# First feed-forward products of groups 1 to 3 as seven block products per pair of jobs instead of eight

## The chip, the cores and the metric

The kernel runs on one core of one Trainium2 chip. The time is that of the device in microseconds; the kernel before took 1534.74 us in the median of 3 runs (1532.2 to 1538.27). In the profile the engines are PE (TensorE, matmuls), PEld (TensorE's loads of the stationary operand), DVE (VectorE), ACT (ScalarE), POOL (GpSimdE) and SP (SyncE, which issues the DMAs).

## The reference

The program is a two-layer trunk over 512 frames with 16 meta tokens set in front of them, so 528 tokens of width 1024. Each layer is a mixer (attention in layer 0, retention in layer 1), and then a feed-forward block with a squared ReLU between two products, each with a scaled residual and a layer norm:

```python
def _sq_relu_mlp(h, w1, w2):
    return jnp.square(jax.nn.relu(h @ w1)) @ w2

for layer in range(DEPTH):
    ...
    h = _layer_norm(DEEPNORM_ALPHA * h + mix, ln_g[layer, 0], ln_b[layer, 0])
    h = _layer_norm(DEEPNORM_ALPHA * h + _sq_relu_mlp(h, ffn_w1[layer], ffn_w2[layer]),
                    ln_g[layer, 1], ln_b[layer, 1])
return h[:, N_META:, :]
```

`w1` is 1024 x 4096 and `w2` 4096 x 1024, everything in float32. The change is in the product `h @ w1`.

## The kernel before

**Layout and precision.** Activations lie transposed: features on the 128 partitions, tokens along the columns. `hs[k]` is feature tile k of 8, as a pair of a high part `hh` and a low part `hl` whose sum is the value. Weights are split the same way, into `wh` and `wl`. Every product takes three passes (PASSES): high by high, high by low, low by high. Layer 0 works on all 528 tokens (FULL) in two halves of 264 columns, layer 1's block on 512 (S_FULL); the meta tokens are not needed after it.

**Weights.** `weight_plan` lists all 224 weight tiles of 128 x 1024 in the order of use. `prepare` (L197 to L207) takes the next one: SP loads `raw` (L203), ScalarE casts it to `wh` (L205), VectorE subtracts to get `wl` (L206). `weights` (L209) keeps this two tiles ahead of the products. The raw tiles have a pool of 3, everything else of this size shares `upool` with 44 buffers.

**The feed-forward block.** `mlp` (L1059) goes through 4 groups of 1024 hidden features. An up job takes one weight tile and yields 128 hidden features. In layer 0 it is 48 matmuls of 264 columns (8 feature tiles, 3 passes, 2 halves) into a two-bank PSUM tile `mm`, in layer 1 it is 24 matmuls of 512 columns into a `bank`. Then `squared` (L1047) applies the ReLU on ScalarE (L1052), the square to the high part `gh` on ScalarE (L1054), and on VectorE the square in full (L1055) and the low part `gl` (L1056). A down job adds one tile of the second product to `y` (L1034, L1036 for the first group). Two up jobs of the next group stand ahead of the eight down jobs of a group, so that TensorE has work while the last squares are made; six follow behind. The last group's down jobs are given to `tail`, which makes the layer norm beside them. PSUM has 2 tiles of two banks (`mm`) and 4 single banks.

**What sets the order.** A scheduler orders the instructions of each engine by the program's order and their operands; each engine then works through its own queue in that order and waits on semaphores of the others. `Ordered` (`pe`) fixes TensorE's order to that of the program where `pe.on` is set.

Of the kernel before, what the change touches and what calls it, by code (L numbers as in the profile page):

```python
# [8 lines left out]
F32 = mybir.dt.float32  # L9
# [39 lines left out]
def weight_plan():  # L49
    plan = []  # L50
    qa, ka, va, qb, kb, vb = (512 * i for i in range(6))

    def wide(name, c0):
        for kk in range(4):
            plan.append(("B", name, 0, 256 * kk, c0))

    def tall(name, c0, r0=0):
        plan.append(("A", name, 0, r0, c0))

    wide("even_w_in", va)  # L60
# [47 lines left out]
    return plan  # L108


@with_exitstack
def kernel(
# [36 lines left out]
            return self.put(nc.tensor.transpose(*a, **k))  # L149
    pe = Ordered()  # L150
    plan = weight_plan()

    cpool = ctx.enter_context(tc.tile_pool(name="cpool", bufs=1))
# [43 lines left out]
    def prepare(load=nc.sync.dma_start):  # L197
        i = queue["next"]
        if i == len(plan):
            return  # L200
        queue["next"] += 1
        raw = rpool.tile([P, 1024], F32, tag="raw", name="raw")
        load(out=raw, in_=w[i])  # L203
        wh, wl = flat(F32R, "wh"), flat(F32R, "wl")
        act.copy(out=wh, in_=raw)  # L205
        dve.tensor_tensor(out=wl, in0=raw, in1=f(wh), op=ALU.subtract)  # L206
        queue["ready"].append((wh, wl))  # L207

    def weights(kind, ahead=2):  # L209
        while queue["next"] < min(len(plan), queue["used"] + 1 + ahead):  # L210
            prepare()
        assert plan[queue["used"]][0] == kind
        queue["used"] += 1
        wh, wl = queue["ready"].pop(0)
        k, n = {"A": (8, P), "B": (2, 512), "C": (4, 256)}[kind]
        return tuple(t.rearrange("p (k n) -> p k n", k=k, n=n) for t in (wh, wl))
# [830 lines left out]
    def squared(dst):  # L1047
# [8 lines left out]
            dve.tensor_tensor(out=gl, in0=s[:, :n], in1=f(gh), op=ALU.subtract)  # L1056
        return put

    def mlp(hs, full, a, b, norm, gs, steps=LN_STEPS):  # L1059
        for g in range(NG):  # L1060
            nxt = []

            def up(into, upto):
                while len(into) < upto:
                    dst = two(F32R, "g")
                    get, run = job(hs, squared(dst))
                    run(get(), full)
                    into.append(dst)
# [4 lines left out]
            if g + 1 < NG:  # L1073
                for get, run in jobs:
                    run(get(), full)
                up(nxt, 8)
            else:
# [247 lines left out]
```

## Time and profile before

| what | number |
|---|---|
| median of 3 runs | 1534.74 us (1532.2 to 1538.27) |
| span of the profiled execution | 1538.6 us |
| stretch of layer 0's feed-forward block that the windows take | 390 to 690 us of the span |
| stretch of layer 1's feed-forward block that the windows take | 1200 to 1480 us of the span |
| weight tiles | 224, of which 64 for `ffn_w1` |

Of the profiled execution only the span is given, no time of its own beside it. The page has the busy time of each engine, the chain of work that ended last, groups of instructions and DMA issues. Rows of the timeline read: start and duration in us, engine, line, operation, result and operands, shape, and in brackets the idle time of the engine before it with what ended that. Rows that group instructions read: how many, busy us and mean ns of one, then the idle time before them with what ended most of it. Windows give the busy time of each engine in a stretch, with the number of instructions in brackets, and the granted clock of TensorE (1.00 is full).

### The profile page before, as it was taken

How to read it: one execution, taken by the hardware profiler on the slowest of the kernel's cores; microseconds unless marked ns; L12 is line 12 of the kernel's file. 1: busy time of each engine (PE TensorE's matmuls, PEld its weight loads, DVE VectorE, ACT ScalarE, POOL GpSimd, SP SyncE). 2: the span in 40 equal slices, each digit the busy share in tenths (PEclk: the TensorE clock that was granted, in tenths of full speed). 3: DMA queues.
4: the chain of work that ended last, by engine and by line, in shares of the span. 5: the costliest groups of instructions: out<-in, count | busy, mean ns of one | idle time of the engine just before them, and what ended most of it. 6: DMA issues, size and time to landing. Idle time of an engine off the chain costs nothing.

```text
span 1538.6 us, 22350 instructions
## 1 busy us (share of the span) xinstructions
PE 1514.1 (98%) x9464; PEld 1343.7 (87%) x9464; DVE 774.2 (50%) x1306; ACT 581.5 (38%) x940; POOL 0.2 (0%) x4
## 2 busy tenths in 40 slices
PE   8999999999999999999999999999999999999997
PEld 6887878799999999999988888888899888888886
DVE  4565466577514435157544354254477524435257
ACT  4474344436403224044444343153455403223133
POOL 0000000000000000000000000000000000000000
PEclk9999999899999999999999999999999999999998
DMA  6111102140302414034013135022150312414021
GB/s 241 56 52 45 56 28 85 44 149 19 129 32 83 137 44 154 31 131 135 28 35 119 36 107 168 0 77 101 46 174 28 122 57 83 137 55 165 28 83 55
DMA packets 39588, 128.97 MB, mean 84 GB/s; under 512 B 4724, under 2 KB 7172, under 8 KB 39488
## 3 DMA queue, kind: packets, MB, share of 16 engines
q1 hardware_dynamic: 39488, 127.54, 25.2%
q8 instruction: 74, 1.21, 0.3%
q14 instruction: 26, 0.21, 0.0%
HBM read 125.43 MB, written 2.10 MB: 83 GB/s over the span
## 4 chain that ended last, share of the span: by engine, by line
PE 97%; DVE 2%; ACT 0%; DMA 0%; issue 0%; ACTq 0%
PE bank L146 45%; PE mm L146 30%; PE v_ps L146 10%; PE s_ps L146 5%; PE o_ps L146 4%; PE t_ps L149 1%; PE sum_ps L146 1%; DVE y L896 0%; PE fb_ps L146 0%; PE mo_ps L146 0%; PE vm_ps L146 0%; PE ms_ps L146 0%; DMA raw<-in_w 0%; PE rows_ps L146 0%; PE sm_ps L146 0%; DVE s L293 0%
## 5 line engine op out<-in xcount | busy, mean ns | idle before, releaser
L206 DVE TENSOR_TENSOR wl<-raw,wh 128x1024 fp32r<-128x1024 f32 x224 | 271.6, 1222 | 92.4 <-ACT wh L205 84.4
L205 ACT CAST wh<-raw 128x1024 fp32r<-128x1024 f32 x224 | 230.5, 1043 | 104.3 <-DMA raw<-in_w 101.9
L146 PE MATMUL bank<-hh,wh 128*128 128x512 f32 (+3 forms) x640 | 220.9, 356 | 0.0
L146 PE MATMUL bank<-hh,wl 128*128 128x512 f32 (+3 forms) x640 | 216.5, 350 | 0.0
L146 PE MATMUL bank<-g,wh 128*128 128x512 f32 (+2 forms) x800 | 200.7, 342 | 0.0
L146 PE MATMUL bank<-hl,wh 128*128 128x512 f32 (+3 forms) x640 | 196.1, 350 | 4.1 <-DVE hl L888 4.1
L146 PEld LDWEIGHTS bank<-g,wh 128*128 128x128 f32 x800 | 137.9, 188 | 18.2
L146 PEld LDWEIGHTS bank<-hh,wh 128*128 128x128 f32 x640 | 120.9, 189 | 18.9 <-ACT hh L900 1.2
L146 PE MATMUL bank<-g,wl 128*128 128x512 f32 (+2 forms) x400 | 136.3, 341 | 0.0
L1055 DVE TENSOR_TENSOR relu<-relu 128x528 f32<-128x528 f32 (+3 forms) x76 | 46.6, 613 | 178.0 <-ACT relu L1052 178.0
L146 PEld LDWEIGHTS bank<-hh,wl 128*128 128x128 f32 x640 | 120.8, 189 | 16.8
L146 PE MATMUL mm<-g,wh 128*128 128x264 f32 x832 | 134.9, 284 | 0.0
L146 PEld LDWEIGHTS bank<-hl,wh 128*128 128x128 f32 x640 | 108.8, 188 | 22.1 <-DVE hl L888 4.7
L146 PEld LDWEIGHTS mm<-g,wh 128*128 128x128 f32 x832 | 115.0, 188 | 0.0
L146 PE MATMUL mm<-hh,wh 128*128 128x264 f32 x512 | 104.1, 285 | 0.0
L146 PE MATMUL mm<-hl,wh 128*128 128x264 f32 x512 | 104.1, 284 | 0.0
L146 PE MATMUL mm<-hh,wl 128*128 128x264 f32 x512 | 103.9, 284 | 0.0
L1052 ACT ACTIVATE relu<-bank 128x512 f32<-128x512 f32 (+2 forms) x50 | 24.7, 493 | 194.4 <-PE bank L146 194.4
L146 PE MATMUL mm<-s,wh 128*128 128x264 f32 x544 | 95.4, 298 | 0.5 <-DVE s L302 0.5
L1052 ACT ACTIVATE relu<-mm 128x528 f32<-128x528 f32 x26 | 15.9, 612 | 189.5 <-PE mm L146 189.5
L146 PE MATMUL mm<-g,wl 128*128 128x264 f32 x416 | 84.3, 284 | 0.0
L146 PEld LDWEIGHTS mm<-s,wh 128*128 128x128 f32 x544 | 77.3, 194 | 6.9 <-issue 2.3
(267 smaller groups left out, 2494.9 us busy)
## 6 DMA issues: line engine op xcount, KB each, us to landing
raw<-in_w SPq DMA_DIRECT2D x224, 512.0 KB, 3.8
xf<-in_x SPq DMA_DIRECT2D x8, 264.0 KB, 5.6
y<-in_x SPq DMA_DIRECT2D x8, 264.0 KB, 4.4
out<-y SPq DMA_DIRECT2D x8, 256.0 KB, 2.2
nb<-in_c_nb SPq DMA_DIRECT2D x4, 264.0 KB
rd<-in_c_rd SPq DMA_DIRECT2D x4, 256.0 KB
rd<-in_c_rm SPq DMA_DIRECT2D x4, 192.0 KB, 3.7
fm<-in_c_fm SPq DMA_DIRECT2D x1, 264.0 KB, 2.7
```

The lines of the kernel that those rows point to most:

```text
L146: return self.put(nc.tensor.matmul(*a, **k))
L149: return self.put(nc.tensor.transpose(*a, **k))
L205: act.copy(out=wh, in_=raw)
L206: dve.tensor_tensor(out=wl, in0=raw, in1=f(wh), op=ALU.subtract)
L1052: act.activation(out=a, in_=ps, func=AF.Relu)
L1055: dve.tensor_tensor(out=s[:, :n], in0=r[:, :n], in1=r[:, :n], op=ALU.mult)
```

## The change

Groups 1 to 3 of the up products, 12 pairs of jobs in each layer, become 12 quads in each layer. A quad takes the two weight tiles of 256 hidden features, cuts the contraction into two halves of 512, the features into two blocks of 128 and the tokens into two halves, which is a 2 x 2 by 2 x 2 block product. In place of the eight block products it makes seven by Strassen's scheme: "11", "a", "b", "12", "d", "c" and "22", each 4 feature tiles in 3 passes, 12 matmuls of 264 (layer 0) or 256 columns (layer 1). The operands "a", "b", "c" and "d" of the weights are sums made in `quad_steps` (below L225 is the subtraction for `wl`, L238 the sum s0, L244 and L246 the sum s1, L249 the low part of the block "12"); those of the tokens are differences made by `combined` once per layer, while group 0's products and down jobs run. The casts to high parts are ScalarE's. The results are put together on VectorE in v (L1163), m (L1165), L1170, L1172 and L1176, with two copies on ScalarE (L1161, L1168); then come ReLU and square in one operation (L1178, 128 x 1056 in layer 0), the cast on ScalarE (L1179) and the low part (L1180). These line numbers are of the changed kernel.

Two accumulators, of "b", "c" and "22" in bank 0 and of "d" in bank 1, share the two-bank PSUM tile `qc`. "22" and what follows it is done inside the next quad (`between`), between its "b" and its "12". One quad of the next group stands ahead of the down jobs of groups 1 and 2, so the quads of a layer run in sequences of 5, 4 and 3. The two weight tiles of a quad are loaded one quad ahead; their preparation goes on by a step after each block product. The raw tiles move to `upool`, which has 46 buffers, and their own pool goes. `pe.on` is set from the first quad to the last but the tail. Host-side packing puts the four blocks of a quad into two tiles, so that as many bytes are loaded as before.

```diff
@@ weight_plan, mlp
+        def quad(g, q):
+            plan.append(("Q", "ffn_w1", layer, 0, D * g + 2 * P * q))
         for g in range(NG):
-            if g + 1 < NG:
-                up(g + 1, 0)
-                up(g + 1, 1)
+            if g and g + 1 < NG:
+                quad(g + 1, 0)
             for f in range(KT):
                 down(g, f)
             if g + 1 < NG:
-                for f in range(2, 8):
-                    up(g + 1, f)
+                for q in range(min(g, 1), 4):
+                    quad(g + 1, q)
...
-    upool = ctx.enter_context(tc.tile_pool(name="upool", bufs=44))
-    rpool = ctx.enter_context(tc.tile_pool(name="rpool", bufs=3))
+    upool = ctx.enter_context(tc.tile_pool(name="upool", bufs=46))
...
+    def halves(raw):
         wh, wl = flat(F32R, "wh"), flat(F32R, "wl")
         act.copy(out=wh, in_=raw)
         dve.tensor_tensor(out=wl, in0=raw, in1=f(wh), op=ALU.subtract)
+        return wh, wl
+
+    def quad_steps(quad, at):
+        lo, hi = slice(0, 512), slice(512, 1024)
+        r0, r1 = flat(F32, "raw"), flat(F32, "raw")
+        nc.sync.dma_start(out=r0, in_=w[at])
+        nc.sync.dma_start(out=r1, in_=w[at + 1])
+        yield
+        h, l = halves(r0)
+        quad["11"], quad["22"] = (h[:, lo], l[:, lo]), (h[:, hi], l[:, hi])
+        yield
+        s0 = flat(F32, "sums")
+        dve.tensor_tensor(out=s0.rearrange("p (a b) -> p a b", a=2), in0=r0.rearrange("p (a b) -> p a b", a=2),
+                          in1=dup(r1[:, hi], 512), op=ALU.add)
+        yield
+        h, l = halves(s0)
+        quad["c"], quad["a"] = (h[:, lo], l[:, lo]), (h[:, hi], l[:, hi])
+        s1 = flat(F32, "sums")
+        dve.tensor_tensor(out=s1[:, lo], in0=s0[:, hi], in1=r0[:, lo], op=ALU.add)
+        yield
+        dve.tensor_tensor(out=s1[:, hi], in0=s1[:, lo], in1=r1[:, lo], op=ALU.add)
+        t = flat(F32R, "w12")
+        act.copy(out=t[:, lo], in_=r1[:, lo])
+        dve.tensor_tensor(out=t[:, hi], in0=r1[:, lo], in1=f(t)[:, lo], op=ALU.subtract)
+        quad["12"] = t[:, lo], t[:, hi]
+        yield
+        h, l = halves(s1)
+        quad["b"], quad["d"] = (h[:, lo], l[:, lo]), (h[:, hi], l[:, hi])
+
+    def advance():
+        for item in queue["ready"]:
+            if isinstance(item, dict) and next(item["steps"], item) is not item:
+                return
...
+    def combined(a, b, into):
+        (c1, n), (c2, _) = a, b
+        for j in range(2):
+            p, q = (y_t[2 * i + j] for i in range(2))
+            p1, p2, q1, q2 = (t[:, :, c:c + n] for t in (p, q) for c in (c1, c2))
+            u, v = (both(F32, "ts")[:, :, :2 * n] for _ in range(2))
+            dve.tensor_tensor(out=u[:, :, :n], in0=p2, in1=p1, op=ALU.subtract)
+            dve.tensor_tensor(out=u[:, :, n:], in0=q2, in1=u[:, :, :n], op=ALU.subtract)
+            yield
+            dve.tensor_tensor(out=v[:, :, :n], in0=p2, in1=q2, op=ALU.subtract)
+            dve.tensor_tensor(out=v[:, :, n:], in0=q1, in1=u[:, :, n:], op=ALU.subtract)
+            yield
+            for t in (u, v):
+                h, l = (both(F32R, "tc")[:, :, :2 * n] for _ in range(2))
+                act.copy(out=h, in_=t)
+                dve.tensor_tensor(out=l, in0=t, in1=f(h), op=ALU.subtract)
+                into.append((h, l))
+                yield
+
+    def quad_up(hs, ts, a, b, dst, between):
+        (c1, n), (c2, _) = a, b
+        quad = weights("Q")
...
+        def multiply(ps, name, xs, first):
+            wt = quad[name]
+            for k in range(4):
+                for i, (p, q) in enumerate(PASSES):
+                    pe.matmul(ps, lhsT=wt[p][:, P * k:P * k + P], rhs=xs[k][q], start=first and k == 0 and i == 0, skip_group_check=not first,
+                              stop=k == 3 and i == 2)
+            advance()
+
+        pa, pb, pcd = bank("qa")[:, :n], bank("qb")[:, :n], two_banks("qc")
+        pc, pd = pcd[:, 0, :n], pcd[:, 1, :n]
+        gh, gl = dst
+        tv = both(F32, "tv").rearrange("p a b -> p (a b)")
+        t, v, m = (tv[:, n * i:n * i + n] for i in range(3))
+        r = both(F32, "up")
+        one, two_ = slice(c1, c1 + n), slice(c2, c2 + n)
+        multiply(pa, "11", plain(0, c1), True)
+        act.copy(out=t, in_=pa)
+        multiply(pb, "a", mixed(0), True)
+        dve.tensor_tensor(out=v, in0=pb, in1=t, op=ALU.subtract)
+        multiply(pc, "b", mixed(1), True)
+        dve.tensor_tensor(out=m, in0=pc, in1=v, op=ALU.add)
+        between()
+        multiply(pa, "12", plain(4, c1), False)
+        act.copy(out=r[:, 0, one], in_=pa)
+        multiply(pd, "d", plain(4, c2), True)
+        dve.tensor_tensor(out=r[:, 0, two_], in0=pd, in1=m, op=ALU.subtract)
+        multiply(pc, "c", mixed(2), False)
+        dve.tensor_tensor(out=r[:, 1, two_], in0=pc, in1=v, op=ALU.add)
+
+        def finish():
+            multiply(pc, "22", mixed(3), False)
+            dve.tensor_tensor(out=r[:, 1, one], in0=pc, in1=t, op=ALU.subtract)
+            rs, hs_, ls = (x[:, :, c1:c1 + 2 * n] for x in (r, gh, gl))
+            dve.scalar_tensor_tensor(out=rs, in0=rs, scalar=0.0, in1=rs, op0=ALU.max, op1=ALU.mult)
+            act.copy(out=hs_, in_=rs)
+            dve.tensor_tensor(out=ls, in0=rs, in1=f(hs_), op=ALU.subtract)
+        return finish
...
         for g in range(NG):
             nxt = []
...
-            up(gs, 8)
-            if g + 1 < NG:
-                up(nxt, 2)
+            if g and g + 1 < NG:
+                quads(nxt, 1)
             jobs = [job(gs, add_into(y[k], ALPHA if g == 0 else None)) for k in range(KT)]
...
+            for k, (get, run) in enumerate(jobs):
+                run(get(), full)
+                if k == 0:
+                    between()
+                advance()
+                advance()
+            pe.on = True
             gs = nxt
+            quads(gs, 4 - len(gs) // 2)
```

**VectorE where layer 0's first down jobs end and the next up jobs begin, before** (`y` is the residual, `relu` is the ReLU's result, `g` a hidden tile, `raw`, `wh` and `wl` the weight tile and its parts; the waits are on semaphores of the named engine or DMA queue):

```order
L206 TENSOR_TENSOR wl<-raw,wh 128x1024 [waits DMAHW3_49,Activation_49]
L206 TENSOR_TENSOR wl<-raw,wh 128x1024 [waits DMAHW4_49,Activation_49]
L1036 SCALAR_TENSOR_TENSOR y<-y,mm 128x528 [waits PE_49]
L206 TENSOR_TENSOR wl<-raw,wh 128x1024 [waits DMAHW5_49,DVE_49,Activation_49]
L1036 SCALAR_TENSOR_TENSOR y<-y,mm 128x528 [waits PE_49] x6
L1055 TENSOR_TENSOR relu<-relu 128x528 [waits Activation_49]
L1056 TENSOR_TENSOR g<-relu,g 128x528 [waits DVE_49,Activation_49]
L206 TENSOR_TENSOR wl<-raw,wh 128x1024 [waits DMAHW6_49,Activation_49]
```

Each up job brings two operations of 528 columns (L1055, L1056), each weight tile one of 1024 (L206), and each down job one of 528 (L1036).

**VectorE in the second quad of the first sequence, after** (numbers tell the tiles apart: `qc_4852`, `tv_4853`, `up_4854`, `g_4845` belong to the first quad, `qb_4960`, `qc_4961`, `tv_4962`, `up_4963` to the second, `wl_5009`, `sums_5012`, `w12_5028`, `wl_5048` and `raw_4955`, `raw_4956` are weights of the third):

```order
L1163 TENSOR_TENSOR tv_4962<-qb_4960,tv_4962 128x264 [waits PE_49,Activation_49]
L1165 TENSOR_TENSOR tv_4962<-qc_4961,tv_4962 128x264 [waits DVE_49,PE_49]
L1176 TENSOR_TENSOR up_4854<-qc_4852,tv_4853 128x264 [waits PE_49]
L225 TENSOR_TENSOR wl_5009<-sums_4993,wh_5008 128x1024 [waits Activation_49]
L244 TENSOR_TENSOR sums_5012<-sums_4993,raw_4955 128x512
L1178 SCALAR_TENSOR_TENSOR up_4854<-up_4854 128x1056 [waits DVE_49]
L249 TENSOR_TENSOR w12_5028<-raw_4956,w12_5028 128x512 [waits Activation_49]
L246 TENSOR_TENSOR sums_5012<-sums_5012,raw_4956 128x512 [waits DVE_49]
L1180 TENSOR_TENSOR g_4845<-up_4854,g_4844 128x1056 [waits Activation_49]
L225 TENSOR_TENSOR wl_5048<-sums_5012,wh_5047 128x1024 [waits Activation_49]
L1170 TENSOR_TENSOR up_4963<-qc_4961,tv_4962 128x264 [waits PE_49]
L225 TENSOR_TENSOR wl_5102<-raw_5080,wh_5101 128x1024 [waits DMAHW7_49,Activation_49]
```

L1170, which reads the second quad's "d", stands behind the first quad's L1176, L1178 and L1180 and behind five operations on the third quad's weights; L1172, which reads "c", follows two further on.

**TensorE at the end of an up job, before** (`mm` is the accumulator; the waits are for the parts of the weight):

```order
L146 MATMUL mm<-hh,wh 128x264 x2
L146 MATMUL mm<-hl,wh 128x264 x2
L146 MATMUL mm<-hh,wl 128x264 x2
L146 MATMUL mm<-hh,wh 128x264 [waits Activation_49]
L146 MATMUL mm<-hh,wh 128x264
L146 MATMUL mm<-hl,wh 128x264 x2
L146 MATMUL mm<-hh,wl 128x264 [waits DVE_49]
L146 MATMUL mm<-hh,wl 128x264
```

Matmuls of consecutive jobs go to different accumulators and wait only for weights.

**TensorE in the second quad of the first sequence, after** (`hh`, `hl` are the tokens' parts, `tc` the tokens' differences; the rows are the last of "d" and the first of "c"):

```order
L156 MATMUL qc_4961<-hh_3332,wh_4935 128x264
L156 MATMUL qc_4961<-hl_3333,wh_4935 128x264
L156 MATMUL qc_4961<-hh_3332,wl_4936 128x264
L156 MATMUL qc_4961<-hh_3332,wh_4935 128x264
L156 MATMUL qc_4961<-hl_3333,wh_4935 128x264
L156 MATMUL qc_4961<-hh_3332,wl_4936 128x264
L156 MATMUL qc_4961<-tc_4335,wh_4899 128x264 [waits DVE_49]
L156 MATMUL qc_4961<-tc_4336,wh_4899 128x264
L156 MATMUL qc_4961<-tc_4335,wl_4900 128x264
L156 MATMUL qc_4961<-tc_4335,wh_4899 128x264
```

The first matmul of "c" waits for a VectorE count that only L1170 of this quad reaches (L1170 reads bank 1 of `qc_4961`, "c" writes bank 0), and no matmul of other work stands between "d" and "c". The first matmul of "d" waits in the same way for L1165, which reads bank 0.

More of the change, by code (lines that the diff above doesn't have):

```diff
@@ L108, in weight_plan, with plan_tiles @@
     return plan
+def plan_tiles(plan):
+    first, n = [], 0
+    for item in plan:
+        first.append(n)
+        n += 2 if item[0] == "Q" else 1
+    return first
 @with_exitstack
@@ L201, in prepare @@
         queue["next"] += 1
-        raw = rpool.tile([P, 1024], F32, tag="raw", name="raw")
-        load(out=raw, in_=w[i])
+        if plan[i][0] == "Q":
+            quad = {}
+            quad["steps"] = quad_steps(quad, first_tile[i])
+            next(quad["steps"])
+            queue["ready"].append(quad)
+            return
+        raw = flat(F32, "raw")
+        load(out=raw, in_=w[first_tile[i]])
+        queue["ready"].append(halves(raw))
+    def halves(raw):
         wh, wl = flat(F32R, "wh"), flat(F32R, "wl")
@@ L213, in weights @@
         queue["used"] += 1
+        if kind == "Q":
+            quad = queue["ready"].pop(0)
+            for _ in quad["steps"]:
+                pass
+            return quad
         wh, wl = queue["ready"].pop(0)
@@ new lines, in mlp, with between, quads @@
+    def mlp(hs, full, a, b, norm, gs, steps=LN_STEPS):
+        ts = []
+        mix = combined(a, b, ts)
+        while len(gs) < 8:
+            dst = two(F32R, "g")
+            get, run = job(hs, squared(dst))
+            run(get(), full)
+            gs.append(dst)
+            for _ in range(4):
+                next(mix, None)
+        run_all(mix)
+        left = {"finish": lambda: None}
+        def between():
+            left["finish"]()
+            left["finish"] = lambda: None
+        def quads(into, n):
+            for _ in range(n):
+                gh, gl = both(F32R, "g"), both(F32R, "g")
+                left["finish"] = quad_up(hs, ts, a, b, (gh, gl), between)
+                into += [(gh[:, i, :], gl[:, i, :]) for i in range(2)]
@@ L1258 @@
     for kind, name, layer, r0, c0 in weight_plan():
+        if kind == "Q":
+            for blocks in (((0, 0), (1, 1)), ((1, 0), (0, 1))):
+                tiles.append(np.concatenate([
+                    given[name][layer][r0 + 512 * k:r0 + 512 * k + 512, c0 + 128 * o:c0 + 128 * o + 128]
+                    .reshape(4, 128, 128).transpose(1, 0, 2).reshape(128, 512) for k, o in blocks], axis=1))
+            continue
         kt, n = {"A": (8, 128), "B": (2, 512), "C": (4, 256)}[kind]
```

25 lines of the change are left out of this document (12 added, 13 removed).

## The prediction

> **What bounds the kernel now.** I read the page first, for its span, its busy times and its chain of work that ended last.
>
> ```profile
> span 1538.6 us, 22350 instructions
> PE 1514.1 (98%) x9464; PEld 1343.7 (87%) x9464; DVE 774.2 (50%) x1306; ACT 581.5 (38%) x940; POOL 0.2 (0%) x4
> PE 97%; DVE 2%; ACT 0%; DMA 0%; issue 0%; ACTq 0%
> raw<-in_w SPq DMA_DIRECT2D x224, 512.0 KB, 3.8
> ```
>
> TensorE is busy for 98% of the span and makes up 97% of the chain. The span is the only time there is for the profiled execution, and it lies 3.9 us above the median of the runs (1534.7), about the distance of the slowest run. I therefore work out a difference against this trace and add it to the median. About 0.5%, 7.7 us, is what a measurement of this kernel can tell from no change.
>
> Then the stretches that the change touches, by the windows (the columns after the length are PE, PEld, DVE, ACT and POOL busy, then the granted clock, the DMA share and GB/s): the feed-forward part of layer 0 and that of layer 1.
>
> ```profile
> 390.00:690.00 300.00, 300.00 (x2469) 300.00 (x2468) 115.70 (x129) 82.09 (x103) 0.00 (x0) 1.00 0.27 89
> 1200.00:1480.00 280.00, 280.00 (x1212) 227.52 (x1211) 110.72 (x129) 80.14 (x105) 0.00 (x0) 1.00 0.28 91
> ```
>
> TensorE has no idle time there at all, and it has the full clock. VectorE works 39% of the time, ScalarE 27 to 29%. So a matmul removed there is worth its whole spacing, and nothing else in these stretches is late today. There is also no wait there that the change could take away: whatever waits it brings are new.
>
> **What is removed.** A pair of up jobs has 2 x 48 = 96 matmuls of 264 columns in layer 0; a quad has 7 x 12 = 84. The spacing comes from the ends of up jobs, as ScalarE's timeline shows them (start, duration, then the idle time before):
>
> ```profile
> 461.15 0.61 ACT L1052 ACTIVATE relu<-mm 128x528 f32<-128x528 f32 x1 [38.54 <-PE mm L146]
> ...
> 502.05 0.61 ACT L1052 ACTIVATE relu<-mm 128x528 f32<-128x528 f32 x1 [3.62 <-PE mm L146]
> 1271.81 0.60 ACT L1052 ACTIVATE relu<-bank 128x512 f32<-128x512 f32 x1 [36.10 <-PE bank L146]
> ...
> 1294.01 0.60 ACT L1052 ACTIVATE relu<-bank 128x512 f32<-128x512 f32 x1 [3.36 <-PE bank L146]
> ```
>
> In layer 0 these are 7 intervals in 40.90 us, 5.843 us a job, 121.7 ns a matmul. A quad then takes 84 x 0.1217 = 10.23 us for 11.69: 1.46 us less, 17.5 us for 12 quads. In layer 1, 4 intervals in 22.20 us give 5.55 us a job (24 matmuls of 512), 11.10 a pair. The 256-column matmuls that replace them appear in the tail's down jobs of 24 matmuls each:
>
> ```profile
> 1491.21 0.42 DVE L1034 TENSOR_TENSOR y<-y,bank 128x256 f32<-128x256 f32 x1 [0.57 <-PE bank L146]
> 1494.03 0.42 DVE L1034 TENSOR_TENSOR y<-y,bank 128x256 f32<-128x256 f32 x1 [2.40 <-PE bank L146]
> 1496.87 0.42 DVE L1034 TENSOR_TENSOR y<-y,bank 128x256 f32<-128x256 f32 x1 [1.23 <-PE bank L146]
> ```
>
> 2.82 and 2.84 us for 24 are 118 ns each, so 84 take 9.91 us: 1.19 less, 14.3 for 12. **Removed: 31.8 us**, 1.32 us a quad. That is the gain if TensorE never waits.
>
> **What is added, and on which engine.** The durations:
>
> ```profile
> L206 DVE TENSOR_TENSOR wl<-raw,wh 128x1024 fp32r<-128x1024 f32 x224 | 271.6, 1222 | 92.4 <-ACT wh L205 84.4 <-PE bank L146 1.9
> L1034 DVE TENSOR_TENSOR y<-y,bank 128x264 f32<-128x264 f32 x12 | 5.1, 424 | 2.4 <-PE bank L146 2.4
> L205 ACT CAST wh<-raw 128x1024 fp32r<-128x1024 f32 x224 | 230.5, 1043 | 104.3 <-DMA raw<-in_w 101.9 <-DVE wl L206 1.3 <-PE bank L146 0.8
> 504.31 3.50 DVE L206 TENSOR_TENSOR wl<-raw,wh 128x1024 fp32r<-128x1024 f32 x3
> 1497.40 2.48 DVE L916 SCALAR_TENSOR_TENSOR y<-sum_ps,y 128x512 f32<-128x512 f32 x4
> ```
>
> Queued back to back, three operations of 1,024 columns take 3.50 us, so each but the last costs 1.14. In the same way one of 512 columns costs 0.60 ((2.48 - 0.68) / 3), one of 1,056 costs 1.17 by its size, and one of 264 costs 0.42 alone and 0.35 queued (the same 0.08 of overlap). On VectorE a quad has weight work of three subtractions wl and one s0 of 1,024 columns, two operations for s1 and one for w12 of 512: 4 x 1.14 + 3 x 0.60 = 6.4 us. Its results add five operations of 264 and two of 1,056: 5 x 0.35 + 2 x 1.17 = 4.1. Together 10.5 us of VectorE in a quad that TensorE would finish in 10.23. ScalarE has three casts of 1,024, one of 512, two copies and one of 1,056, about 3 x 1.04 + 0.6 + 0.8 + 1.08 = 5.6 us. So VectorE, 39% busy before, becomes as loaded as TensorE.
>
> A load alone would cost little. What costs is where TensorE waits for it. Product c writes one bank of the tile qc and may start only when VectorE's L1170, which reads d's result in the other bank, is done; nothing else stands on TensorE between d and c. The best case is a wait with an idle VectorE. The two latencies are in these rows of the timeline (PE's last matmul and the operation that it releases; a VectorE operation and the matmul that it releases):
>
> ```profile
> 1505.48 0.29 PE L146 MATMUL bank<-g,wl 128*128 128x256 f32 x1
> 1505.81 0.42 DVE L1034 TENSOR_TENSOR y<-y,bank 128x256 f32<-128x256 f32 x1 [1.50 <-PE bank L146]
> 1525.86 0.43 DVE L928 TENSOR_TENSOR sq<-sq 128x256 f32<-128x256 f32 x1
> 1526.35 0.91 PE L146 MATMUL sum_ps<-sq,ones 128*128 128x256 f32 x3 [0.17 <-DVE sq L928]
> ```
>
> From the last matmul's start to VectorE's start it is 0.33 us, the operation takes 0.42, and 0.06 later TensorE starts: 0.81 in place of a spacing of 0.12, and with some 0.1 for the refilled pipe about **0.8 us a quad at least**.
>
> But VectorE works through its queue in order, and in front of L1170 it has the weight work of the next quad and the result of the quad before. Per quad of a run (a run is what stands between two groups of down products: 5, 4 and 3 quads in each layer):
>
> - First of a run: nothing is queued, 0.8 us.
> - Second of a run. T is the start of the last matmul of the earlier quad's product 22. TensorE is ready for c 24 matmuls later, at T + 3.0. VectorE starts L1176 at T + 0.3 and then has L1176 0.35, wl 1.14, s1 0.60, the squaring L1178 1.17, w12 0.60, s1 0.60, L1180 1.17 and wl 1.14, in all 6.8; L1170 takes 0.42, and c starts at T + 7.6. With the refill **4.7 us**.
> - Middle quads. A is the start of the last matmul of product a. c could start 48 matmuls on, at A + 6.0. VectorE runs from A + 0.3: L1163 0.35, wl 1.14, s1 0.60, L1165 0.35, w12 0.60, L1176 0.35, s1 0.60, L1178 1.25, then it must wait for ScalarE's cast (1.08 and two handovers of 0.05), then L1180 1.17, wl 1.14, L1170 0.42: c starts at A + 9.5 or 9.6. **3.7 us**, and since the next quad's A follows 36 matmuls after c, this repeats in each.
> - Last of a run: no more weight work is queued, but L1176, L1178, the cast and L1180 are (0.35 + 1.25 + 1.18 + 1.17 from T + 0.3, then 0.42): T + 4.8 for T + 3.0, **1.9 us** with the refill.
> - Last of the run of 3: down matmuls stand between d and c, so the wait falls on 22 (0.8), and then the down products need this quad's squares, which go through L1176, L1178, cast and L1180 with nothing else to do: 0.3 + 0.42 + 1.25 + 1.18 + 1.17, **4.3**.
>
> The run of 5: 0.8 + 4.7 + 3.7 + 3.7 + 1.9 = 14.8. The run of 4: 0.8 + 4.7 + 3.7 + 1.9 = 11.1. The run of 3: 0.8 + 4.7 + 5.1 = 10.6. A layer 36.5, both **73 us**. Layer 1's operations are 3% smaller, which I leave out. As bounds for these waits: 24 x 0.8 = 19 us if the queue were never in front, and above by the half clock below.
>
> What costs nothing: the token combinations, some 11 us of VectorE a layer, stand among group 0's products and down jobs, where it is idle 60% of the time, and the first quad needs them 84 matmuls (10 us) after the up jobs end; without that cover they would cost up to those 11 us a layer. The raw tiles are as many as before (224), and each is issued a quad ahead, over 10 us, against 3.8 us to landing.
>
> **The clock.** Today TensorE's longest idle times in work of this kind are these (PE's timeline with two rows that follow each, then three windows):
>
> ```profile
> 350.08 0.51 PE L146 MATMUL bank<-hl,wh 128*128 128x264 f32 x2 [1.37 <-DVE hl L888]
> 350.42 0.28 PE L146 MATMUL bank<-hh,wh 128*128 128x264 f32 x1
> 350.54 0.28 PE L146 MATMUL bank<-hh,wl 128*128 128x264 f32 x1
> 727.70 0.68 PE L146 MATMUL bank<-hl,wh 128*128 128x248 f32 x2 [1.39 <-DVE hl L888]
> 728.18 0.42 PE L146 MATMUL bank<-hh,wh 128*128 128x248 f32 x1
> 728.40 0.42 PE L146 MATMUL bank<-hh,wl 128*128 128x248 f32 x1
> 727.70:729.70 2.00, 2.00 (x9) 1.89 (x9) 1.57 (x4) 2.00 (x7) 0.00 (x0) 0.54 0.03 8
> 730.70:731.20 0.50, 0.50 (x5) 0.50 (x3) 0.50 (x2) 0.50 (x2) 0.00 (x0) 0.50 0.00 0
> 731.20:732.20 1.00, 1.00 (x10) 1.00 (x10) 1.00 (x3) 1.00 (x2) 0.00 (x0) 0.96 0.00 0
> ```
>
> After 1.37 us the spacing is 0.12; after 1.39 us, elsewhere, it is 0.22, with a granted clock of 0.50 to 0.54 until 731.2: half the clock for 3.5 us. Gaps of 3.7 us and more are far longer than either, so I charge each of the 14 (3 + 2 + 2 a layer) with what 3.5 us at 0.22 for 0.12 lose, 1.6 us: **22 us**. The loss lies between c and a, from which the next wait counts, so it adds. Bounds: 0 if the clock holds, and, if the half clock lasts over all 36 matmuls from c to A (4.4 us more each instead of 1.6), 61 us. If gaps of 1.9 us drop it too, as the 1.39 did, four more are charged, 6 us.
>
> The Trainium skill, "TensorE: Matmul & The Clock Gate", section "Why this matters for your kernels", asks for no idle gap of TensorE above about 3 us, because one window of idleness brings half rate. The row at 727.70 shows half rate after 1.39 us, so here the measurement is stricter than the page. By the page only the 14 long gaps cost clock, which gives the sum below; by that row alone the four of 1.9 us do too, which gives 6 us more.
>
> **The sum.** 1534.7 - 31.8 + 73 + 22 = 1598 us.
>
> **Rivals.**
>
> - The clock holds. For: 350.08. Against: 727.70, and gaps more than twice as long. 1534.7 - 31.8 + 73 = 1576. Chance 0.22.
> - The clock stays at half from c to a at every long gap: 1576 + 61 = 1637. For: TensorE never again works 10 us without a gap. Against: the 3.5 us of the trace. Chance 0.08.
> - The other side: VectorE keeps ahead, its weight work fits into TensorE's time and L1170 is never queued behind it, so each quad waits only for the bank, 24 x 0.8 = 19: 1534.7 - 31.8 + 19 = 1522, faster. For: the load of 10.5 us nearly fits into 10.2. Against: the order puts that work ahead of L1170. The point that decides is the mean wait of a quad: under 1.32 us the change gains. Chance 0.06.
> - In between, the waits and the gain cancel within 7.7 us, which needs a mean wait of 1.0 to 1.6 us. Chance 0.04.
>
> **How the numbers follow.** The forecast keeps 0.60. Its own bounds, and the case of a clock that holds, set the range: from 1576 less 1 us for each of the 18 waits that are queued behind weight work (their operands may come sooner than I lay them out), 1558, to 1598 plus 6 for the short gaps and 1 us more for each of the 18, 1622. Left out are the two cases below and the one above, 0.18. Faster 0.06, same 0.04, slower 0.90.
>
> **What would show it.** Right: in the changed profile TensorE's waits name DVE's up L1170 above all others, some 20 times a few us; TensorE's busy share falls to about 93%; the windows of the quads show VectorE near 80% busy and a granted clock under 1; a middle quad's period, from one L1170 to the next, is about 14 to 15.5 us. Step by step: 84 matmuls at a spacing of 0.12 between waits, the combinations without a wait of TensorE for tc, and no idle time put down to raw. Wrong: if the periods are 10 to 11 us, the queue was no wait; if the period is 14 with a clock of 1.00, the clock term falls; if TensorE waits for weights (wh or wl) instead, the place is another.

## The result, and the profile after

The changed kernel takes 1657.8 us (median of 4 runs, 1655.3 to 1663.9); the kernel before took 1536.5 in the runs beside it. The ratio is 1.0794 (95% interval 1.0760 to 1.0827): 121 us slower, where the prediction had 63 us and a range up to 1622. The profiled execution, at 1663.9 us, is the slowest of the four.

The page's lines that answer to those shown of before: the span, the busy times, the clock in 40 slices, and the chain of work that ended last.

```profile
span 1662.1 us, 23173 instructions
PE 1543.5 (93%) x9752; PEld 1385.1 (83%) x9752; DVE 924.6 (56%) x1522; ACT 607.5 (37%) x972; POOL 0.2 (0%) x4
PEclk9979999989998999999999999999989998989988
PE 86%; DVE 10%; ACT 2%; issue 2%; DMA 0%; ACTq 0%; DVEq 0%
```

VectorE is now 10% of the chain. The clock dips in the quads, and also in the third slice, far ahead of the first quad. The view of waits says what TensorE waited for (total, times, longest, all in us):

```profile
PE qc L156 <- DVE up L1170: 57.3, 22, 4.5
PE sum_ps L156 <- DVE acc L909: 21.3, 4, 6.7
PE mm L156 <- ACT g L1179: 3.0, 1, 3.0
PE bank L156 <- ACT g L1179: 2.9, 1, 2.9
```

The first, third and fourth rows are the forecast ones: product c behind L1170, and each layer's last quad. The second row is not in the prediction at all. It is the sum of the layer norm, in the four tails, to which the change adds no operation.

**A middle quad.** VectorE's L1170 of the second to fourth quad of the first run and TensorE's first matmuls of c in the third, as the timeline has them:

```profile
487.77 0.43 DVE L1170 TENSOR_TENSOR up<-qc,tv 128x264 f32<-128x264 f32 x1
504.06 0.42 DVE L1170 TENSOR_TENSOR up<-qc,tv 128x264 f32<-128x264 f32 x1
520.71 0.42 DVE L1170 TENSOR_TENSOR up<-qc,tv 128x264 f32<-128x264 f32 x1
504.54 0.81 PE L156 MATMUL qc<-tc,wh 128*128 128x264 f32 x2 [3.44 <-DVE up L1170]
505.15 0.42 PE L156 MATMUL qc<-tc,wl 128*128 128x264 f32 x1
505.37 0.64 PE L156 MATMUL qc<-tc,wh 128*128 128x264 f32 x2
521.19 0.81 PE L156 MATMUL qc<-tc,wh 128*128 128x264 f32 x2 [3.47 <-DVE up L1170]
534.72 0.52 PE L156 MATMUL qc<-tc,wh 128*128 128x264 f32 x2 [1.70 <-DVE up L1170]
```

The last two rows are the first of c in the fourth and in the fifth quad. The windows: five us from c's start in the third quad and two us later on, the same for the fourth quad (three us, then two), two us of the fifth, and the whole first run:

```profile
504.50:509.50 5.00, 4.96 (x22) 4.96 (x23) 2.68 (x3) 0.00 (x0) 0.00 (x0) 0.50 0.00 0
511.00:513.00 2.00, 2.00 (x19) 2.00 (x18) 1.01 (x2) 1.12 (x2) 0.00 (x0) 1.00 0.00 0
521.00:524.00 3.00, 2.81 (x13) 2.81 (x13) 1.27 (x2) 0.00 (x0) 0.00 (x0) 0.50 0.00 0
524.50:526.50 2.00, 2.00 (x19) 2.00 (x18) 0.17 (x1) 0.38 (x1) 0.00 (x0) 1.00 0.66 166
534.70:536.70 2.00, 1.98 (x16) 1.98 (x17) 0.21 (x1) 0.50 (x1) 0.00 (x0) 1.00 0.59 236
470.00:530.00 60.00, 48.12 (x336) 47.26 (x335) 38.41 (x53) 18.32 (x25) 0.00 (x0) 0.86 0.16 53
```

The wait is 3.4 us, where 3.7 were forecast. Then 22 matmuls run in 5 us at a granted clock of 0.50, and the spacing of 0.22 lasts until about 510.4, 5.9 us and not 3.5. The period is 16.3 and 16.65 us, where the forecast had 14 to 15.5, with 1.6 for the clock. Behind the fourth quad's wait, which is as long, the clock is back at 1.00 by 524.5, after about 3.1 us. Behind the fifth quad's 1.70 us it did not fall.

**A tail.** The first layer norm of layer 0: VectorE's queue in front of the sum and TensorE's wait for it, in the timeline of after,

```profile
341.48 0.43 DVE L1092 SCALAR_TENSOR_TENSOR y<-y,bank 128x264 f32<-128x264 f32 x1 [1.36 <-PE bank L156]
344.41 0.43 DVE L1092 SCALAR_TENSOR_TENSOR y<-y,bank 128x264 f32<-128x264 f32 x1 [1.37 <-PE bank L156]
345.90 0.70 DVE L916 TENSOR_TENSOR acc<-y 128x528 f32<-128x528 f32 x1
348.12 0.43 DVE L909 TENSOR_TENSOR acc<-acc 128x264 f32<-128x264 f32 x1
348.61 1.25 PE L156 MATMUL sum_ps<-acc,ones 128*128 128x264 f32 x2 [4.23 <-DVE acc L909]
```

and the window of that stretch:

```profile
335.00:352.00 17.00, 12.77 (x90) 12.35 (x90) 11.97 (x17) 1.34 (x3) 0.00 (x0) 0.85 0.19 62
```

The timeline of before at the same place,

```profile
324.64 0.70 DVE L862 TENSOR_TENSOR acc<-acc,y 128x528 f32<-128x528 f32 x1
328.85 0.43 DVE L1036 SCALAR_TENSOR_TENSOR y<-y,bank 128x264 f32<-128x264 f32 x1 [2.48 <-PE bank L146]
329.31 0.71 DVE L864 TENSOR_TENSOR acc<-acc,y 128x528 f32<-128x528 f32 x1
331.78 0.43 DVE L1036 SCALAR_TENSOR_TENSOR y<-y,bank 128x264 f32<-128x264 f32 x1 [1.29 <-PE bank L146]
341.03 0.43 DVE L1036 SCALAR_TENSOR_TENSOR y<-y,bank 128x264 f32<-128x264 f32 x1 [0.29 <-PE bank L146]
```

and its window:

```profile
322.00:341.00 19.00, 19.00 (x156) 18.93 (x155) 14.17 (x23) 4.35 (x6) 0.00 (x0) 1.00 0.26 80
```

(The row at 341.03 belongs to the other half, behind the first sum.) Before, the additions into `acc` stood between the residuals (L1036) of the half that was being computed, in time for TensorE's sum. After, all of them stand behind the last of these residuals (the first at 345.90 us), and TensorE is idle for 4.2 us. So VectorE's order moved in a part of the program that the change's new code does not touch. The attention shows it too, by its clock: the window of before,

```profile
90.00:118.00 28.00, 25.93 (x194) 22.70 (x192) 18.75 (x51) 20.47 (x42) 0.00 (x0) 1.00 0.24 74
```

and the one after that holds about as many matmuls (201 for 194):

```profile
90.00:130.00 40.00, 34.78 (x201) 30.07 (x200) 18.26 (x51) 21.39 (x42) 0.00 (x0) 0.77 0.21 65
```

### The profile page after: what moved, and what is told of

Its sections match the earlier page's. It is cut to its first block, busy times and chain, and to the rows that moved or that the text cites. A ratio compares the mean times of both kernels' runs of the same rounds, so it can differ in the third digit from the quotient of the medians.

```text
span 1662.1 us, 23173 instructions
## 1 busy us (share of the span) xinstructions
PE 1543.5 (93%) x9752; PEld 1385.1 (83%) x9752; DVE 924.6 (56%) x1522; ACT 607.5 (37%) x972; POOL 0.2 (0%) x4
## 4 chain that ended last, share of the span: by engine, by line
PE 86%; DVE 10%; ACT 2%; issue 2%; DMA 0%; ACTq 0%; DVEq 0%
PE bank L156 34%; PE mm L156 19%; PE v_ps L156 10%; PE qc L156 7%; PE s_ps L156 4%; PE o_ps L156 4%; PE qa L156 3%; PE qb L156 2%; DVE wl L225 2%; DVE up L1178 1%; DVE g L1180 1%; PE sum_ps L156 1%; PE t_ps L159 1%; ACT g L1179 1%; DVE up L1170 1%
## 5 line engine op out<-in xcount | busy, mean ns | idle before, releaser
L225 DVE TENSOR_TENSOR wl<-raw,wh 128x1024 fp32r<-128x1024 f32 x200 | 240.7, 1218 | 35.1 <-ACT wh L224 35.1
L156 PE MATMUL qc<-tc,wh 128*128 128x264 f32 (+1 forms) x576 | 122.0, 311 | 58.4 <-DVE up L1170 57.3
L156 PEld LDWEIGHTS qc<-tc,wh 128*128 128x128 f32 x576 | 99.7, 211 | 63.6 <-DVE up L1170 61.9
L156 PE MATMUL bank<-hh,wh 128*128 128x512 f32 (+3 forms) x448 | 146.8, 342 | 0.9 <-ACT hh L956 0.8
L156 PE MATMUL bank<-hh,wl 128*128 128x512 f32 (+3 forms) x448 | 141.8, 332 | 0.0
L156 PE MATMUL bank<-hl,wh 128*128 128x512 f32 (+3 forms) x448 | 121.4, 332 | 4.1 <-DVE hl L944 4.1
L156 PEld LDWEIGHTS bank<-hh,wl 128*128 128x128 f32 x448 | 85.4, 191 | 8.5
L156 PE MATMUL qc<-tc,wl 128*128 128x264 f32 (+1 forms) x288 | 88.0, 306 | 0.0
L156 PEld LDWEIGHTS bank<-g,wl 128*128 128x128 f32 x400 | 77.5, 194 | 11.0 <-DVE wl L225 1.8
L156 PEld LDWEIGHTS bank<-hl,wh 128*128 128x128 f32 x448 | 73.3, 189 | 13.7 <-DVE hl L944 4.7
L224 ACT CAST wh<-sums 128x1024 fp32r<-128x1024 f32 x48 | 50.3, 1047 | 86.0 <-DVE sums L238 63.9
L1179 ACT CAST g<-up 128x1056 fp32r<-128x1056 f32 (+1 forms) x24 | 25.4, 1060 | 153.5 <-DVE up L1178 153.5
```

The costliest lines, as they stand in the source:

```text
L156: return self.put(nc.tensor.matmul(*a, **k))
L1179: act.copy(out=hs_, in_=rs)
```

## The experiments

Theory P: what is lost outside the quads comes from one small part of the change, the raw weight tiles in the shared pool. Theory V: what the quads lose is c's wait behind VectorE's queue, with the half clock after it. Rivals stand with each run. Ratios are to runs of the kernel before on the same chip, whose medians were 1537.1 to 1540.0 us.

### The buffer change alone

In the kernel before:

```diff
-    upool = ctx.enter_context(tc.tile_pool(name="upool", bufs=44))
-    rpool = ctx.enter_context(tc.tile_pool(name="rpool", bufs=3))
+    upool = ctx.enter_context(tc.tile_pool(name="upool", bufs=46))
-        raw = rpool.tile([P, 1024], F32, tag="raw", name="raw")
+        raw = flat(F32, "raw")
```

> The kernel before with only the buffer change: the raw weight tiles come from the shared pool of 46 buffers, their own pool of 3 is gone; no quads. Theory P (the 50 us that the changed kernel loses outside its quads come from the raw tiles in the shared pool, which moves instructions in the attention and in the four layer-norm tails): about 1536 + 50, 1575 to 1590 us, with TensorE waiting for the layer norm's sums some 5 to 7 us in each of the four tails. Rival Q (they come from the quads themselves, their order or what the clock makes of them): 1530 to 1545 us.

1585.1 us, ratio 1.0314 (1.0278 to 1.0349), with no quad in the program. The wait for the layer norm's sum is the changed kernel's to a tenth:

```profile
PE sum_ps L146 <- DVE acc L852: 21.3, 4, 6.7
```

and the attention's clock falls as it does there:

```profile
90.00:130.00 40.00, 33.57 (x200) 29.00 (x199) 20.54 (x56) 21.35 (x46) 0.00 (x0) 0.83 0.18 56
```

The residuals that stand at 331.78 and 341.03 us before, ahead of the first sum and behind it, come 6.8 and 13.6 us later in this run:

```profile
338.58 0.43 DVE L1035 SCALAR_TENSOR_TENSOR y<-y,bank 128x264 f32<-128x264 f32 x1 [1.36 <-PE bank L146]
354.60 0.43 DVE L1035 SCALAR_TENSOR_TENSOR y<-y,bank 128x264 f32<-128x264 f32 x1 [0.70 <-PE bank L146]
```

P holds: 48 of the 121 us are the pool's.

### The raw tiles back in a pool of their own

In the changed kernel:

```diff
-    upool = ctx.enter_context(tc.tile_pool(name="upool", bufs=46))
+    upool = ctx.enter_context(tc.tile_pool(name="upool", bufs=44))
+    rpool = ctx.enter_context(tc.tile_pool(name="rpool", bufs=3))
-        raw = flat(F32, "raw")
+        raw = rpool.tile([P, 1024], F32, tag="raw", name="raw")
```

> The changed kernel with the plain raw tiles back in a pool of 3 of their own and 44 shared buffers (the raw tiles of the quads stay in the shared pool). Theory P: the 50 us outside the quads go, 1658 - 50 = 1608 us, 1600 to 1618, and no wait for the layer norm's sums above 1 us; the waits for up L1170 stay at 55 to 60 us in all. Rival Q: 1650 to 1665 us.

1607.8 us, ratio 1.0449 (1.0396 to 1.0502): 50 us less than the changed kernel, and the sum's wait is gone from the list, while L1170's stays.

```profile
PE qc L156 <- DVE up L1171: 59.2, 22, 4.5
PE v_ps L156 <- ACT s L349: 6.0, 1, 6.0
```

(A line is inserted above, so L1170 has the number L1171. The second row stood in the profile of before with 5.9.) So the quads cost 70.7 us by this run, and 72.7 by the run before it (1657.8 - 1585.1). The forecast for them was 63.

### Is it the number of buffers?

In the kernel with the buffer change alone:

```diff
-    upool = ctx.enter_context(tc.tile_pool(name="upool", bufs=46))
+    upool = ctx.enter_context(tc.tile_pool(name="upool", bufs=47))
```

> The kernel before with only the buffer change, but 47 shared buffers in place of 46, as many tiles as the 44 and 3 before. If the number of buffers is what the reordering comes from, 1530 to 1545 us; if it is that raw tiles take turns with all others in one pool, 1578 to 1592 us as with 46.

1585.5 us, ratio 1.0312 (1.0285 to 1.0339). With as many tiles as 44 and 3 nothing comes back: it is the sharing, not the one tile less. More than 47 were not tried.

### The layer norm's sum out of the shared pool

Again in the kernel with the buffer change alone:

```diff
+    apool = ctx.enter_context(tc.tile_pool(name="apool", bufs=1))
...
     def layer_norm(span, li, hs):
-        acc = both(F32, "acc")[:, :, :n]
+        acc = apool.tile([P, 2, L], F32, tag="acc", name="acc")[:, :, :n]
```

> The kernel before with the buffer change alone (46 shared buffers, raw tiles among them), and the layer norm's sum acc in a buffer of its own. Theory T (in the shared pool acc takes its turn behind the raw tiles that were asked for before it, so its additions go late on VectorE): the additions come early again, TensorE's waits for sum_ps behind acc (21.3 us, 4 times) go nearly all, and of the 48 us about 30 come back, leaving the attention's 14: 1548 to 1560 us. Rival U (the additions go late for another reason, or the next tile of the shared pool, the squares, keeps the same place): 1575 to 1590 us.

1592.8 us, ratio 1.0339 (1.0322 to 1.0356): nothing comes back, the second case of the rival, and the time is 3 us above even its range. But the waits tell more than the time:

```profile
PE sum_ps L146 <- DVE sq L853: 19.1, 4, 6.3
PE sum_ps L146 <- DVE acc L853: 6.7, 3, 3.8
```

`acc`'s wait falls from 21.3 to 6.7 us, and the squares `sq`, the next tiles that the layer norm takes from the shared pool, now cause 19.1. In the first tail the additions into `acc` stand early again (at 328.08, 333.46 and 339.31 us), and the wait moves to the next tile of the shared pool. That fits theory T's mechanism, although its forecast of the time fell. How the scheduler comes to this order was not traced further.

### Product d in a bank of its own

In the changed kernel:

```diff
-        pa, pb, pcd = bank("qa")[:, :n], bank("qb")[:, :n], two_banks("qc")
-        pc, pd = pcd[:, 0, :n], pcd[:, 1, :n]
+        pa, pb, pd, pc = bank("qa")[:, :n], bank("qb")[:, :n], bank("qd")[:, :n], two_banks("qc")[:, 0, :n]
```

> The changed kernel with product d in a bank of its own, so that c no longer waits for VectorE's reading of d. Theory V (the wait of c behind VectorE's queue, with the half clock after it, is what the quads lose): the 57 us of waits for up L1170 go and most of the half clock with them, and what remains is VectorE's load of 10.5 to 11.5 us a quad: 24 quads from about 14.8 us to about 12, -60 to -70, 1590 to 1605 us. Rival H (only the handover of 0.8 us is the bank's, the rest is VectorE's load and comes back as another wait): -19, about 1639 us.

1584.1 us, ratio 1.0309 (1.0273 to 1.0345): 74 us less than the changed kernel, more than V expected. What is left in a middle quad of the first run is an L1170 (here L1169) every 11.6 us, at full clock, with VectorE busy for 26.09 of 30 us and small waits for the low parts. In layer 1's run of 5 it is every 12.8 us; why was not traced.

```profile
PE qc L156 <- DVE wl L225: 9.0, 12, 0.8
```

and the window of three quads:

```profile
470.00:500.00 30.00, 28.48 (x227) 27.70 (x226) 26.09 (x36) 12.93 (x17) 0.00 (x0) 1.00 0.26 82
```

V's mechanism holds, though the time lies 6 us below its range, and H falls. The wait is the program's: c and d use different banks, but one tile, and a tile is what the semaphores know.

### Idle work in the gap

In the changed kernel, ahead of product c:

```diff
+    FILL, filled = (0, 24, 24, 24, 8, 0, 24, 24, 8, 0, 24, 0), [0]
...
+        fill = FILL[filled[0] % 12]
+        filled[0] += 1
+        if fill:
+            spare = bank("qx")[:, :n]
+            for k in range(fill):
+                pe.matmul(spare, lhsT=quad["11"][0][:, :P], rhs=hs[0][0][:, c1:c1 + n], start=k == 0, stop=k == fill - 1)
         multiply(pc, "c", mixed(2), False)
```

> The changed kernel with idle work for TensorE between d and c in the quads with a long wait: 24 matmuls into a bank that nobody reads (8 in two shorter ones, none in the others); the output is unchanged. Theory C (after each long gap TensorE runs c and what follows at half clock, 2.6 us lost each time, on the path): the granted clock stays at 1.00 in the quads, -25 to -36 us, 1622 to 1633, although more matmuls run. Rival N (the clock after the gaps does not lie on the path, the queue of VectorE sets the period anyway): no gain, 1655 to 1670 us.

1631.5 us, ratio 1.0617 (1.0579 to 1.0656): 320 matmuls more, and 26 us less than the changed kernel. The timeline of a filled gap:

```profile
490.51 3.05 PE L156 MATMUL qx<-hh,wh 128*128 128x264 f32 x24
494.12 0.51 PE L156 MATMUL qc<-tc,wh 128*128 128x264 f32 x2 [0.56 <-DVE up L1172]
```

and the window of the first run:

```profile
470.00:530.00 60.00, 56.08 (x456) 55.24 (x455) 38.84 (x52) 18.57 (x25) 0.00 (x0) 1.00 0.27 88
```

The first rows are the third quad's filler and what is left of its wait; the clock of the first run is 1.00 where the changed kernel's was 0.86. The waits for L1170 (here L1172) are shorter by 37 us, about what the 320 matmuls take at 0.12 us each (38):

```profile
PE qc L156 <- DVE up L1172: 20.4, 22, 1.7
```

In every gap with filler part of the wait is left, so no filler outlasts it, and what the kernel gains is the clock. C holds: the half clock after the gaps lies on the path.

### Both costs taken out

The second and the fifth edit together (own pool for raw tiles, own bank for d).

> Both costs taken out of the changed kernel: plain raw tiles in a pool of 3 of their own with 44 shared buffers, and product d in a bank of its own. If the two causes are separate, their gains add: 1658 - 50 - 74 = 1534 us, 1526 to 1542, no difference from the kernel before that can be told. If they overlap (the reordered tails hide part of the quads' loss), 1545 to 1575.

1538.8 us, ratio 1.0003 (0.9985 to 1.0021). The gains add, within 5 us: 1657.8 - 50.0 - 73.7 = 1534. What the quads still lose then takes as much as the 31.8 us that the fewer matmuls save. Of that, 9.0 us are TensorE's waits for the low parts and 4.9 those for the last squares; the rest was not separated.

### Towards a faster version

GpSimd for three operations of a quad, from the kernel with both costs taken out (the diff shows one; those of `s1[:, hi]` and `t[:, hi]` are moved in the same way):

```diff
-        dve.tensor_tensor(out=s1[:, lo], in0=s0[:, hi], in1=r0[:, lo], op=ALU.add)
+        nc.gpsimd.tensor_tensor(out=s1[:, lo], in0=s0[:, hi], in1=r0[:, lo], op=ALU.add)
```

> As the kernel with both costs undone, and three operations of a quad's weight work (the two of s1 and the low part of block 12, 128 x 512 each) on GpSimd in place of VectorE, 1.8 us less of VectorE in a quad. Theory V (VectorE's load of 10.5 us and its handovers set the middle quads' 11.6 us): the period falls to 10.2 to 10.6 us, -15 to -25, 1510 to 1520 us. Rival G (GpSimd's operations are slow or slow VectorE's, and TensorE waits for the weights of b and d): no gain or a loss, 1534 to 1570 us.

1529.0 us, ratio 0.9941 (0.9921 to 0.9962): 0.6% under the kernel before, and 10 us under the kernel that it starts from, not 15 to 25. That lies between the ranges of both theories, and the gain is not where V expected it. The middle period is 11.2 us in layer 0, but 12.7 to 13.0 in layer 1, where it was 11.5 to 12.8 without GpSimd. What was gained is in the second quads of the six runs: their L1170 follows that of the first quad after 13.7 to 13.9 us in place of 15.4 to 15.7. GpSimd's and VectorE's operations stand in each other's way, as their rows show:

```profile
457.20 1.29 POOL L250 TENSOR_TENSOR w<-raw,w 128x512 fp32r<-128x512 f32 x1 [0.30 <-POOL sums L245]
458.45 2.31 POOL L247 TENSOR_TENSOR sums<-sums,raw 128x512 f32<-128x512 f32 x1
458.16 1.45 DVE L1178 SCALAR_TENSOR_TENSOR up<-up 128x1056 f32<-128x1056 f32 x1
459.53 2.31 DVE L226 TENSOR_TENSOR wl<-sums,wh 128x1024 fp32r<-128x1024 f32 x1
462.94 1.21 DVE L226 TENSOR_TENSOR wl<-sums,wh 128x1024 fp32r<-128x1024 f32 x1
```

Alone an operation of 512 columns takes GpSimd 1.29 us and one of 1,024 takes VectorE 1.21; beside each other both take 2.31. GpSimd's of 458.45 begins under VectorE's L1178, which ends at 459.61.

The sums first, in place of GpSimd, again from the kernel with both costs taken out:

```diff
+        s1 = flat(F32, "sums")
+        dve.tensor_tensor(out=s1[:, lo], in0=s0[:, hi], in1=r0[:, lo], op=ALU.add)
+        dve.tensor_tensor(out=s1[:, hi], in0=s1[:, lo], in1=r1[:, lo], op=ALU.add)
         yield
         h, l = halves(s0)
         quad["c"], quad["a"] = (h[:, lo], l[:, lo]), (h[:, hi], l[:, hi])
-        s1 = flat(F32, "sums")
-        dve.tensor_tensor(out=s1[:, lo], in0=s0[:, hi], in1=r0[:, lo], op=ALU.add)
         yield
-        dve.tensor_tensor(out=s1[:, hi], in0=s1[:, lo], in1=r1[:, lo], op=ALU.add)
+        h, l = halves(s1)
+        quad["b"], quad["d"] = (h[:, lo], l[:, lo]), (h[:, hi], l[:, hi])
+        yield
         t = flat(F32R, "w12")
         act.copy(out=t[:, lo], in_=r1[:, lo])
         dve.tensor_tensor(out=t[:, hi], in0=r1[:, lo], in1=f(t)[:, lo], op=ALU.subtract)
         quad["12"] = t[:, lo], t[:, hi]
-        yield
-        h, l = halves(s1)
-        quad["b"], quad["d"] = (h[:, lo], l[:, lo]), (h[:, hi], l[:, hi])
```

> As the kernel with both costs undone (1539 us), with the steps of a quad's weight work in another order: both operations of s1 directly after s0, the casts and low parts behind them, block 12 last; nothing on GpSimd. Theory W (1.2 us of a middle quad's 11.6 are VectorE waiting for ScalarE's cast of s1, the rest is its load): the period falls to 10.4 to 10.8 us, -10 to -18, 1521 to 1529 us. Rival L (the load alone sets it, the wait only moves): 1535 to 1542 us.

1526.7 us, ratio 0.9920 (0.9891 to 0.9948). The time is as expected, and TensorE's waits for the low parts fall from 9.0 us to 0.5. But the expected sign, an L1170 every 10.4 to 10.8 us, did not show in the first run of quads: the scheduler gave VectorE yet another order, with L1170 up to 13 us apart, and three waits for L1165:

```profile
PE qc L156 <- DVE tv L1165: 5.9, 3, 3.5
PE bank L156 <- ACT g L1179: 2.9, 1, 2.9
PE mm L156 <- ACT g L1179: 2.0, 1, 2.0
PE qc L156 <- DVE wl L226: 0.5, 1, 0.5
```

Over both layers the middle period is 11.5 to 13.4 us, for 11.5 to 12.8 with both costs taken out. The gain is again in the second quads, whose L1170 follows the first quad's after 12.6 to 13.0 us in place of 15.4 to 15.7. So the forecast time came out without the step that it rested on, which is luck, and theory W is not shown.

Two plain jobs for each layer's last quad, on top of that (the plan of weights gets the two up jobs in the place of the last quad of group 3):

```diff
-            quads(gs, 4 - len(gs) // 2)
+            quads(gs, 4 - len(gs) // 2 - (g + 2 == NG))
+            while g + 2 == NG and len(gs) < 8:
+                dst = two(F32R, "g")
+                get, run = job(hs, squared(dst))
+                run(get(), full)
+                between()
+                gs.append(dst)
```

> As the one with the sums first, and the last pair of each layer made by two plain up jobs in place of a quad, so that the last down products don't wait for a quad's squares. Two quads less: +1.46 and +1.19 us; TensorE's waits of 3.0 and 2.9 us for the last squares go, with the half clock behind them 1 to 2 us each: -4 to -8, 1515 to 1525 us. If those waits only move to the next operand, no change from the one before.

1519.6 us, ratio 0.9865 (0.9833 to 0.9898), the fastest of all, 18 us under the kernel before. The two waits for the squares in the rows above are gone from its list; those for L1165 (here L1168) stay, so this is not yet the end.

## Why the prediction was wrong

**The direction and the mechanism in the quads were right.** c waits for L1170 behind VectorE's queue in 22 of 24 quads, the middle wait is 3.4 us (3.7 forecast), and the last quad's squares are waited for (3.0 and 2.9 us, 4.3 forecast). L1170's 57.3 us and the squares' 5.9 are 63 of the 73 forecast. The token combinations and the raw loads made no wait for TensorE in the lists, as forecast. TensorE's share is the 93% forecast, though the tails' waits, which were not forecast, are in it; VectorE's, 38.4 of 60 us in the first run, is 64% and not near 80%. The rival in which VectorE keeps ahead needed less than 1.32 us a quad; the mean was 2.4 for L1170 alone.

**The step that failed is "what costs nothing".** The prediction counted the raw tiles as loads, "as many as before (224)", found them issued early enough, and went on. It costed the change of the pool at nothing and took the rest of the program at the times of before. The run with that change alone shows 48 us for it, and without it the changed kernel is 50 us faster: four tails in which the layer norm's tiles come late on VectorE, and an attention with more idle time and a lower clock. In the run with that change alone the residual ahead of the first tail's wait is 6.8 us late and the one behind it 13.6 (338.58 and 354.60 us in the rows above); the other three tails bring most of the rest. The attention's part differs between executions: with the same buffers, the residual of 331.78 us stands at 344.41 in the changed kernel's profile, 12.6 later, and at 336.24, 4.5 later, in the one with a bank for d, where the window from 90 to 130 us has a clock of 0.91 and not 0.77. That the order moved there stood in the program's order on VectorE before any run. The prediction looked only at the places around the new code. The attention's share is shown to come from the pool; which of its moved instructions starts the half clock was not separated.

**One term was too small: the clock.** The prediction gave 22 us, 1.6 for each of 14 gaps. The half clock did come 14 times in the quads: at the 12 long waits for L1170 and at the two for the squares, and at none of the four waits of 1.7 us. But it lasted longer: windows over these stretches show a granted clock of 0.50 for 6.8 us in eight of them, 3.4 in five and 10.2 in one. TensorE is busy for 69 us of that, which at a spacing of 0.22 for 0.12 loses about 31 us. Filling the 12 long gaps, which removes their half clock and shortens nothing else, gave 26 back; the 58 us behind these 12 lose 26 by the same sum. The prediction's duration came from one gap of 1.39 us. The rivals "the clock holds" and "half from c to a at every gap" were both off; the bound of the second, 4.4 us a gap, should have been 3.6 by the prediction's own spacings (36 matmuls at 0.22 for 0.12).

Sum: 48 for the pool, 65.5 of waits (L1170, the squares, and 2.3 in rows of 1.0 us and less) and 31 for the clock, less 31.8, make 113 of the 121. The other 8 us are not placed by these runs.

## What to carry to other kernels

When a change puts tiles into a pool that others use, compare the order of every engine over the whole program, not just around the new code: here a change that adds no operation cost 48 us in places that nobody edited. A product that waits for a reader of another bank of the same tile waits by bookkeeping alone; one tile for each accumulator took 74 us away. And an idle TensorE costs more than its gap: add what the half clock takes behind it, with a range, since waits of the same length here brought 3 us of it or 6.

## What the runs showed of the hardware

- The half clock lasted 3.5 us after a gap of 1.39 us in the trace of before. In the changed kernel's quads it came at every wait for L1170 of 3.4 to 4.5 us and at none of the four of 1.7. Its length did not follow the wait's: TensorE ran at half for 5.9 us behind a wait of 3.44 us, and for about 3.1 behind one of 3.47. Work that nobody needs, put into the gaps, held the clock at 1.00 and made the kernel 26 us faster.
- VectorE's and GpSimd's operations on SBUF held each other up: 1.21 and 1.29 us alone, 2.31 each where they met. In the rows above GpSimd's ends at 460.76 and VectorE's, issued at 459.53, ends 1.08 later, about its full duration. The Trainium skill, "SBUF — State Buffer", section "Who interferes with whom", says that the two share a port pair under an exclusive lock, and that a VectorE instruction with two inputs in SBUF contends with a GpSimd instruction that reads SBUF. The rows agree: L226 and L247 both read two tiles in SBUF.
